# Strassen's scheme in the output projection of a hybrid streaming encoder layer

## The chip, the cores and the metric

The kernel runs on one core of one Trainium2 chip. The metric is the device time of an execution in microseconds (us). All arithmetic is float32: each operand of a large product is split into a high half (its cast to the type float32r) and a low half (what the cast leaves), and TensorE multiplies high by high, low by high and high by low. A product of a 128 x 128 stationary tile with 512 columns therefore takes three matmuls.

## The reference, cut to what matters

One layer works on 2048 prompt tokens and 64 sample tokens of width 1024. Three groups of heads (HGRN2 of width 1024, retention of width 512, attention to a memory of width 512) give `mixed`, whose width is 2048. What the change touches is the end of the layer:

```python
    mixed = jnp.concatenate([o_hg, o_rt, o_xa], axis=-1)      # (tokens, 2048)
    out = x.astype(f32) + mixed @ w_out.astype(f32)           # w_out (2048, 1024)
...
y_prompt = rms_norm(hp, final_norm_g)   # hp: out of the prompt tokens
y_sample = rms_norm(hs, final_norm_g)   # hs: out of the sample tokens
```

## The kernel before, in words

**Order of the work.** The kernel projects the normalised tokens to all heads (helpers `gemm_col`, whose matmuls are line 249, and `gemm_tok`, line 294), works through the head groups, and writes each gated group to a DRAM buffer `mixT` (2048 features x 2112 tokens). Last among the groups is the attention to the memory, `xa_heads`; its products are lines 741, 763 and 785, and its gates lines 422 and 423. The output projection follows. Two engines run in exactly the order in which the program is written: TensorE, and SyncE, which issues all loads and stores. For the others a scheduler puts instructions in order; those written under `tc.high_priority` are drawn forward.

**A clock of its own.** `pe(us)` counts TensorE's time in the program, and `poll()` issues the steps of background generators whose time has come. `store(dst, src)` is such a task: its DMA (line 127) is placed in SyncE's queue 4.5 us, by this count, after the call.

**Weights.** `wsrc` lists 512 KB slabs (128 x 1024). `w_fetch` loads a slab into one of three buffers `st` (line 141), `w_pump` splits it (`split`, lines 240 and 241: ScalarE casts the high half, VectorE subtracts for the low one) into a pair of buffers `whi`, `wlo`, or, for the output projection, also into the buffers `ha` and `hb`, which held normalised tokens. `worder` assigns the 16 slabs of `w_out` to these: five to `whi`/`wlo`, four to `ha`, four to `hb`, and the rest to `whi`/`wlo` and eight small buffers. All of `w_out`, both halves, stays in the core's memory while the output runs. `allow["a"]` opens `ha` during the last attention head, `allow["b"]` opens `hb` after it.

**The output stage.** For each of 16 chunks of 128 tokens (and the sample's 64 before the last one) `y_load` splits the chunk's 16 tiles of `mixT` as stationary operands (four splits of 512 columns) and loads x. `y_half` runs once for each half of the output's columns: 16 contraction tiles x 3 terms = 48 matmuls (line 1159) into one bank of PSUM, then VectorE adds x (line 1168) and ScalarE squares and sums (line 1169). The two norms' sums give a factor per token, with GpSimd's power in between, and VectorE scales by it and by `final_norm_g` (lines 1182 and 1185). `mix_fetch` (line 1005) asks for the next chunk's `mixT` between the two halves, and x follows (line 1030). For the sample the high and low halves stand side by side in one stationary tile, so that a product needs two matmuls: 64 in all.

Of the kernel before, what the change touches and what calls it, by code (L numbers as in the profile page):

```python
# [15 lines left out]
P = 128  # L16
# [18 lines left out]
E_OFF = [0, 128, 224, 288]  # L35

# [27 lines left out]
def layer_kernel(ctx: ExitStack, tc: tile.TileContext, io: dict):  # L64
# [6 lines left out]
    mvd = tc.dram_tile([NMEM, 512], F32, name="mvd")  # L71

# [22 lines left out]
    def task(cls, gen, delay):  # L95
        prev = last.get(cls)
        t = {"t": now[0] + delay, "gen": gen, "prev": prev, "stage": 0}
        last[cls] = t
        pend.append(t)
# [34 lines left out]
    wpos = {"dma": 0, "split": 0, "credit": 0, "ahead": 1}  # L134
    allow = {}

    def w_fetch(now_=0):
        while wpos["dma"] < min(len(wsrc), wpos["split"] + max(now_, wpos["ahead"])):
            i = wpos["dma"]
            wst[i] = stp.tile([P, 1024], F32, tag="st", name="wst")  # L140
            dma(wst[i], wsrc[i][0])
            wpos["dma"] += 1

    def w_pump():
        while wpos["split"] < len(wsrc):
            i = wpos["split"]
            n, tag = wsrc[i][1:]
            if tag == "w":
                if not wpos["credit"]:
                    break  # L150
                wpos["credit"] -= 1
                hi = wpool.tile([P, 1024], F32R, tag="whi", name="whi")
                lo = wpool.tile([P, 1024], F32R, tag="wlo", name="wlo")
            elif tag == "v":
                if tag not in allow:
                    break
                w_fetch()
                parts_ = [[vpool.tile([P, 512], F32R, tag="v", name="v") for _ in range(2)] for _ in range(2)]
                st = wst.pop(i)
                for k in range(2):  # L160
                    split(parts_[0][k], parts_[1][k], st[:, k * 512:(k + 1) * 512])
                wt[i] = parts_
# [3 lines left out]
            else:  # L166
                if tag not in allow:
                    break
                if not allow[tag]:
                    allow[tag] += [allow_alloc(tag), 0]  # L170
                (hi_, lo_), j = allow[tag]
                allow[tag][1] += 1
                hi, lo = hi_[:, j * 1024:(j + 1) * 1024], lo_[:, j * 1024:(j + 1) * 1024]
# [5 lines left out]

    def allow_alloc(tag):  # L180
        return [t.rearrange("p k n -> p (k n)") for t in h_tile(tag)]
# [14 lines left out]
    cst = const.tile([P, 396], F32, name="cst")  # L196
# [5 lines left out]
    ones = const.tile([P, P], F32, name="ones")  # L202
# [15 lines left out]
    s_prompt = [const.tile([P, P], F32, name=f"sp{h}") for h in range(8)]  # L218
# [4 lines left out]
    def small(n, tag):  # L223
        return sm.tile([P, n], F32, tag=tag, name=tag, bufs=2 if n == 32 else 3)
# [501 lines left out]
    def att_tail(h, tok0, nt, kv_p, kv_s, qh, ql, sh):  # L726
# [48 lines left out]
        po = acc()  # L775
# [70 lines left out]
    n_in = len(wsrc)  # L846
    worder = [(0, i, "w") for i in range(4)] + [(0, i, "a") for i in range(4, 8)] + [(1, 0, "w")]
    worder += [(1, i, "b") for i in range(1, 5)] + [(1, 5, "w"), (1, 6, "v"), (1, 7, "v")]
    wsrc += [(io["w_out_t"][half, i], 512, tag) for half, i, tag in worder]
# [146 lines left out]
    def mix_fetch(o, L, early):  # L996
        out = []
        for q in range(0, 4, 1 if early else 2):
            if early:
                m = vpool.tile([P, 512], F32, tag="v", name="mv").rearrange("p (k l) -> p k l", k=4)  # L1000
                n = 1
            else:
                m = stp.tile([P, 1024], F32, tag="st", name="mst").rearrange("p (k l) -> p k l", k=8)
                n = 2
            dma(m[:, :, 0:L], mixT[q * 512:(q + n) * 512, o:o + L].rearrange("(k p) l -> p k l", p=P))
# [280 lines left out]
```

## Time and profile before

| | |
|---|---|
| median of 3 runs | 1949.01 us (1948.51 to 1950.47) |
| profiled execution | 1948.53 us, span 1946.7 us |
| granted TensorE clock, mean | 0.993 |
| TensorE matmuls busy | 1912.0 us (98%), 10938 |
| VectorE busy | 1043.7 us (54%) |
| ScalarE busy | 586.5 us (30%) |
| GpSimd busy | 140.6 us (7%) |
| DMA | 153.21 MB, mean 79 GB/s |

The span is the time from the first to the last instruction that the profiler recorded; the execution's own time is 1.8 us longer. In the profile PE is TensorE's matmuls, PEld its weight loads, DVE VectorE, ACT ScalarE, POOL GpSimd, SP SyncE. A row such as `L1159 PE MATMUL acc<-whi,s` names the line of the kernel, the engine, and the output and the inputs by the program's names. A number in brackets at its end is the idle time ahead of it and what ended it. The share of the DMA engines is the mean over the core's 16.

### The profile page before, as it was taken

Reading aid. Unit: us, or ns where it says so; the run is one execution under the profiler, and the core shown is the slowest. Engines: PE = TensorE matmul, PEld = TensorE weight load, DVE = VectorE, ACT = ScalarE, POOL = GpSimd, SP = SyncE. Lnnn points to the kernel's source line nnn. Section 1 sums busy time; section 2 is a strip of 40 time slices with the busy share of each in tenths; the row PEclk is TensorE's granted clock in tenths of the full one; section 3 lists DMA queues with packets and bytes.
Section 4 is the critical chain, followed back from the end, with each engine's and each line's share of the span. In section 5 each row is a group of like instructions: output and inputs, shape, how many; then the busy total and the mean of one; then the engine's idle time right before and its main releaser. Section 6 shows DMA issues by size and latency. Waiting matters only on the chain.

```text
span 1946.7 us, 28118 instructions
## 1 busy us (share of the span) xinstructions
PE 1912.0 (98%) x10938; PEld 1620.4 (83%) x10938; DVE 1043.7 (54%) x2512; ACT 586.5 (30%) x1414; POOL 140.6 (7%) x335
## 2 busy tenths in 40 slices
PE   8999999999999999999999999999999999999998
PEld 7888788888888787987789998899988978888886
DVE  7616547762767546417737775477765652222222
ACT  6412232232233434412323332233334431111111
POOL 0000100000100100000101111021100000000000
PEclk8999999999999999999999999999999999999999
DMA  7512211111111413411311111111122352233322
GB/s 253 172 59 55 81 55 52 63 44 49 44 44 60 147 60 121 126 54 49 96 48 46 53 49 49 44 49 49 60 71 73 104 162 87 87 100 110 93 71 60
DMA packets 116742, 153.21 MB, mean 79 GB/s; under 512 B 13312, under 2 KB 79232, under 8 KB 116608
## 3 DMA queue, kind: packets, MB, share of 16 engines
q1 hardware_dynamic: 116608, 151.41, 25.3%
q8 instruction: 86, 1.41, 0.3%
q14 instruction: 48, 0.39, 0.1%
HBM read 117.69 MB, written 33.69 MB: 78 GB/s over the span
## 4 chain that ended last, share of the span: by engine, by line
PE 88%; DVE 5%; DMA 2%; ACT 2%; issue 1%; POOL 1%; SPq 0%; DVEq 0%; POOLq 0%; ACTq 0%
PE acc L249 39%; PE acc L1159 19%; PE acc L294 16%; PE scb L522 2%; PE ob L531 2%; PE ob L563 1%; PE ob L566 1%; PE acc L264 1%; PE acc L785 1%; PE ob L741 1%; DVE wlo L241 1%; PE tr L516 1%; PE tr L763 1%; PE tr L581 1%; POOL rs L237 0%
## 5 line engine op out<-in xcount | busy, mean ns | idle before, releaser
L249 PE MATMUL acc<-hb,whi 128*128 128x320 f32 (+2 forms) x1696 | 410.8, 332 | 0.4 <-DVE hb L371 0.4
L249 PE MATMUL acc<-ha,whi 128*128 128x512 f32 x1120 | 353.2, 396 | 0.0
L249 PEld LDWEIGHTS acc<-hb,whi 128*128 128x128 f32 x1696 | 285.8, 190 | 25.3 <-issue 4.4
L241 DVE TENSOR_TENSOR wlo<-wst,whi 128x1024 fp32r<-128x1024 f32 x118 | 143.8, 1226 | 266.3 <-ACT whi L240 265.3
L249 PE MATMUL acc<-hb,wlo 128*128 128x256 f32 (+2 forms) x848 | 277.7, 327 | 0.0
L249 PEld LDWEIGHTS acc<-ha,whi 128*128 128x128 f32 x1120 | 204.2, 188 | 41.1 <-issue 2.6
L249 PE MATMUL acc<-ha,wlo 128*128 128x512 f32 x560 | 219.4, 392 | 0.0
L240 ACT CAST whi<-wst 128x1024 fp32r<-128x1024 f32 x118 | 122.8, 1051 | 209.7 <-PE acc L249 172.0
L249 PEld LDWEIGHTS acc<-hb,wlo 128*128 128x128 f32 x848 | 160.9, 190 | 11.3
L294 PE MATMUL acc<-whi,ha 128*128 128x512 f32 x512 | 161.5, 397 | 0.0
L294 PE MATMUL acc<-whi,hb 128*128 128x512 f32 x512 | 160.0, 394 | 0.0
L1159 PE MATMUL acc<-whi,s 128*128 128x512 f32 x396 | 125.8, 396 | 1.3 <-ACT s L240 1.0
L249 PEld LDWEIGHTS acc<-ha,wlo 128*128 128x128 f32 x560 | 105.3, 188 | 22.7
L294 PEld LDWEIGHTS acc<-whi,hb 128*128 128x128 f32 x512 | 94.5, 188 | 19.8 <-issue 1.2
L294 PEld LDWEIGHTS acc<-whi,ha 128*128 128x128 f32 x512 | 94.1, 189 | 19.6 <-issue 1.3
L294 PE MATMUL acc<-wlo,ha 128*128 128x512 f32 x256 | 100.1, 391 | 0.0
L294 PE MATMUL acc<-wlo,hb 128*128 128x512 f32 x256 | 99.8, 390 | 0.0
L1159 PE MATMUL acc<-ha,s 128*128 128x512 f32 x400 | 96.3, 396 | 0.0
L1159 PE MATMUL acc<-hb,s 128*128 128x512 f32 x400 | 96.2, 396 | 0.0
L241 DVE TENSOR_TENSOR s<-mst,s 128x512 fp32r<-128x512 f32 (+1 forms) x64 | 40.4, 672 | 97.2 <-ACT s L240 97.2
L1159 PEld LDWEIGHTS acc<-whi,s 128*128 128x128 f32 x396 | 74.3, 188 | 19.6 <-ACT s L240 1.3
L1159 PEld LDWEIGHTS acc<-ha,s 128*128 128x128 f32 x400 | 75.0, 188 | 18.2
(234 smaller groups left out, 2915.5 us busy)
## 6 DMA issues: line engine op xcount, KB each, us to landing
wst<-w_in_t SPq DMA_DIRECT2D x104, 512.0 KB, 3.8
mixT<-s SPq DMA_DIRECT2D x64, 256.0 KB, 4.2
mst<-mixT SPq DMA_DIRECT2D x30, 512.0 KB, 5.7
wst<-w_out_t SPq DMA_DIRECT2D x16, 512.0 KB, 4.0
xq<-x_prompt SPq DMA_DIRECT2D x18, 256.0 KB, 4.9
o_yp<-xq SPq DMA_DIRECT2D x18, 256.0 KB, 2.1
s<-mixT SPq DMA_DIRECT2D x16, 256.0 KB, 3.1
s<-x_prompt SPq DMA_DIRECT2D x16, 256.0 KB, 5.1
```

Source lines behind the costliest of these rows:

```text
L240: S.copy(hi, src)
L241: V.tensor_tensor(out=lo, in0=src, in1=hi.bitcast(F32), op=ALU.subtract)
L249: T.matmul(ps[:, 0:nt], w[a][:, kk, :], ht[b][:, kk, 0:nt], start=(n == 0), stop=(n == 23))
L264: T.matmul(ps[:, 0:nt], w[a][:, kk, :], ht[b][:, kk, 0:nt], start=(kk == 0 and a + b == 0), stop=(kk == KT - 1 and a == 1))
L294: T.matmul(ps[0:L, :], ht[b][:, kk, o:o + L], w[a][:, kk % 2, :], start=(n == 0), stop=(n == 23))
L516: T.transpose(trk[:, c * 128:(c + 1) * 128], kch[:, c * 128:(c + 1) * 128], ident)
L522: T.matmul(scb[32 * e:32 * e + 32, c * 128 + 32 * e:(c + 1) * 128], K[:, c * 128 + 32 * e:c * 128 + 32 * e + 32], Qe[:, c, E_OFF[e]:E_OFF[ ...
L531: T.matmul(db[:, c * 128:(c + 1) * 128], kT[:, c * 128:(c + 1) * 128], vt[c], start=True, stop=True)
L563: T.matmul(ob[:, c * 128:(c + 1) * 128], A[:, c * 128:(c + 1) * 128], vt[c], start=True, stop=first)
L566: T.matmul(ob[:, c * 128:(c + 1) * 128], qst[:, c * 128:(c + 1) * 128], st[c][0], start=False, stop=True)
L581: T.transpose(tro[:, c * 128:(c + 1) * 128], on[:, c * 128:(c + 1) * 128], ident)
L1159: T.matmul(ps, m[a][:, kk % 4], w[b], start=(n == 0), stop=(n == 16 * len(terms) - 1))
```

## The change

**What it computes.** The contraction of 2048 is taken in two passes p of 1024. In each pass the token chunks of 128 are taken in pairs. A pair's operand is a matrix of 2 x 2 blocks: a11 and a12 are the two halves (512 each) of the first chunk's contraction, a21 and a22 those of the second chunk. The weights of the pass are B11, B12, B21, B22 (512 x 512 each). Then

```
S1 = a21 + a22   S2 = S1 - a11   S3 = a11 - a21   S4 = a12 - S2
T1 = B12 - B11   T2 = B22 - T1   T3 = B22 - B12   T4 = B21 - T2
P1 = a11 B11  P2 = S2 T2  P3 = S1 T1  P4 = S3 T3  P5 = a12 B21  P6 = a22 T4  P7 = S4 B22
y11 = P1 + P5            y12 = P1 + P2 + P3 + P7
y21 = P1 + P2 + P4 + P6  y22 = P1 + P2 + P3 + P4
```

Each product is 4 contraction tiles x 3 terms = 12 matmuls. They are made in the order B11, T2, T1, T3, B21, T4, B22 (named by the weight block). The sample uses B11, T1, B21, B22, 32 matmuls a pass. The sequence is 8 pairs and the sample in the first pass, then 7 pairs, the sample and the last pair in the second.

**What it moves.** The first pass starts from x, its sums go to a new DRAM buffer `yd`, and the second pass reads them back and does norm, scaling and output. Only one pass's weight blocks fit. Those of the first are built from the slabs at the end of the attention (the functions `o_...`, called by `w_pump`). Those of the second are built during the first pass by `w2_steps`, some seven steps in each pair from the second on: a slab is loaded, blocks are subtracted, and high and low halves of 512 columns go through two pairs of small buffers `wbuf` to DRAM, `wcd`. `w2_load` loads each block from there when the last pair of the first pass, or its sample, has read the same block of the first pass for the last time: T2, T3 and T4 in the last pair, B11, T1, B21 and B22 in the sample. Smaller edits go with it: one product of the last attention head goes to another PSUM bank, `cst` and `ones` become one tile, and so do the eight `s_prompt`, so that x and the sums find room there.

The core of the diff, with the lines of the new kernel that the prediction speaks of named behind it:

```diff
 def w_fetch(now_=0):
-        while wpos["dma"] < min(len(wsrc), wpos["split"] + max(now_, wpos["ahead"])):
+        lim = wpos["split"] + max(now_, wpos["ahead"])
+        if wpos["hold"] is not None:
+            lim = min(lim, wpos["hold"] + 3)
+        while wpos["dma"] < min(len(wsrc), lim):
...
+    def t2_unit(region, u, z, t1):
+        hi, lo = out_unit(region, "T2", u)
+        v2 = [vpool.tile([P, 512], F32, tag="v", name="t2") for _ in range(2)]
+        for k in range(2):
+            c = slice(k * 512, (k + 1) * 512)
+            sub(v2[k], z[:, c], t1[:, c])
+            split(hi[:, c], lo[:, c], v2[k])
+        live["T2", u] = v2
...
+    def o_b21(u):
+        def f(i, x):
+            split(*out_unit("b", "B21", u), x)
+            v2 = live.pop(("T2", u))
+            for k in range(2):
+                c = slice(k * 512, (k + 1) * 512)
+                sub(x[:, c], x[:, c], v2[k])
+            split(*out_unit("b", "T4", u), x)
...
-    nxt = y_load(0, raw0)
     allow["b"] = []
-    allow["v"] = []
     w_pump()
...
+    def a_prep(raw, tmp=None):
+        a11, a12, a21, a22 = raw
+        s1, s2, s4 = tmp or [vpool.tile([P, 512], F32, tag="v", name="as") for _ in range(3)]
+        A = {"B11": part(a11)}
+        vadd(s1, a21, a22)
+        yield A
+        sub(s2, s1, a11)
+        A["T2"] = part(s2)
+        yield A
...
+    def w2_steps():
+        for u in range(2):
...
+            def out(blk, x):
+                for k in range(2):
+                    c = slice(k * 512, (k + 1) * 512)
+                    hi, lo = wbuf[wb[0] % 2]
+                    wb[0] += 1
+                    S.copy(hi, x[:, c])
+                    V.tensor_tensor(out=lo, in0=x[:, c], in1=hi.bitcast(F32), op=ALU.subtract)
+                    yield
+                    dma(wcd[blk][u, 0][:, c], hi.bitcast(F32))
+                    dma(wcd[blk][u, 1][:, c], lo.bitcast(F32))
+
+            x, y, z = load("B11"), load("B12"), load("B22")
+            yield
+            sub(y, y, x)
+            sub(z, z, y)
+            sub(x, z, x)
+            yield
+            yield from out("T3", x)
+            yield from out("T1", y)
+            v = load("B21")
+            yield
+            sub(v, v, z)
+            yield from out("T2", z)
+            yield from out("T4", v)
+            for blk in ("B11", "B21", "B22"):
+                x = load(blk)
+                yield
+                yield from out(blk, x)
+
+    def w2_load(blk):
+        for u in range(2):
+            for i in range(2):
+                dma(wo[blk, u][i].bitcast(F32), wcd[blk][u, i])
...
+        prod(Z, "T1", A["T1"], True, True)
+        with hp():
+            vadd(r[3], r[3], Z)
+            vadd(r[1], r[1], Z)
+        if 0 < n < len(seq) - 1:
+            r_next = r_fetch_next()
+        prep()
...
+        if last1:
+            w2_load("T4")
```

In the new kernel `sub` is line 168, `vadd` line 1207, the two halves of `split` lines 314 and 315, the matmuls of `prod` line 1252, the low halves of `w2_steps` line 1272, the loads of `w2_load` line 1298, `mixT` is asked for on line 1080, and all other stores are line 130.

Three places in the order of the engines. First VectorE, where the output stage starts; before, the last gate of the attention (`s<-s,acc`) and the first token splits (`s<-mv,s`) stand so:

```order
L241 TENSOR_TENSOR wlo<-wst,whi 128x1024
L241 TENSOR_TENSOR s<-acc,s 128x320
L423 SCALAR_TENSOR_TENSOR s<-s,acc 128x320
L241 TENSOR_TENSOR s<-mv,s 128x512
L241 TENSOR_TENSOR hb_14563<-wst,hb_14562 128x1024
L241 TENSOR_TENSOR s<-mv,s 128x512
```

And now, with the first and the second product's token splits at the end (`sp_all` holds S2):

```order
L315 TENSOR_TENSOR wlo<-wst,whi 128x1024
L497 SCALAR_TENSOR_TENSOR s<-s,acc 128x320
L315 TENSOR_TENSOR hb_14554<-wst,hb_14553 128x1024 x2
L168 TENSOR_TENSOR wst<-wst,t_14117 128x512
L168 TENSOR_TENSOR wst<-wst,t_14118 128x512
L168 TENSOR_TENSOR wst<-wst,t_14371 128x512
L168 TENSOR_TENSOR wst<-wst,t_14372 128x512
L315 TENSOR_TENSOR wlo<-wst,whi 128x1024
L315 TENSOR_TENSOR hb_14554<-wst,hb_14553 128x1024 x2
L315 TENSOR_TENSOR s<-mv,s 128x512
L315 TENSOR_TENSOR s<-sp_all,s 128x512 x2
```

The splits of the last slabs (B21 into `hb`, B22 into `wlo`) and the four subtractions for T4 have come to stand between the gate and the first token split; before, one `hb` split stood behind it.

Second VectorE in the middle of the output stage; before, one chunk's rows follow the other's (L241 token splits, L1168 adds, L1182 and L1185 norm and scaling):

```order
L241 TENSOR_TENSOR s<-mst,s 128x512 x4
L1168 TENSOR_TENSOR xq<-xq,acc 128x512 x2
L1182 TENSOR_TENSOR rs_15347<-ss_15220 128x1
L1185 SCALAR_TENSOR_TENSOR xq<-xq,rs_15347,q2b_138 128x512
L1185 SCALAR_TENSOR_TENSOR xq<-xq,rs_15347,q2b_139 128x512
L241 TENSOR_TENSOR s<-mst,s 128x512 x4
L1168 TENSOR_TENSOR abuf_109<-abuf_109,acc 128x512
L1168 TENSOR_TENSOR abuf_111<-abuf_111,acc 128x512
```

And now in the first pass, from the add of the fifth pair's third product (T1) on; `wst` are slabs of the second pass, `hb` and `q2b` the buffers `wbuf`, `abuf` and `m` the sums, `as` and `mv` token blocks:

```order
L1207 TENSOR_TENSOR xq<-xq,acc 128x512
L168 TENSOR_TENSOR wst<-wst 128x1024 x3
L1272 TENSOR_TENSOR hb_14553<-wst,hb_14553 128x512
L1272 TENSOR_TENSOR q2b_138<-wst,hb_14554 128x512
L1272 TENSOR_TENSOR hb_14553<-wst,hb_14553 128x512
L1207 TENSOR_TENSOR abuf_116<-abuf_116,m_15432 128x512
L315 TENSOR_TENSOR s<-mv,s 128x512
L1207 TENSOR_TENSOR m_15432<-m_15432,acc 128x512
L1207 TENSOR_TENSOR abuf_116<-abuf_116,tr 128x512
L1207 TENSOR_TENSOR abuf_118<-abuf_118,m_15432 128x512
L1207 TENSOR_TENSOR as<-mv 128x512
L1207 TENSOR_TENSOR abuf_118<-abuf_118,acc 128x512
```

Three wide subtractions and three low halves of weights stand ahead of the token split `s<-mv,s` of the same pair.

Third SyncE. Before, the middle of the output stage repeats this, loads of the next chunk and stores of the one before:

```order
L1030 DMA abuf_111<-x_prompt 128x512
L127 DMA o_yp<-xq 128x512 x2
L1005 DMA mst<-mixT 128x8x128 x2
L1030 DMA xq<-x_prompt 128x512 x2
L127 DMA o_yp<-abuf_109 128x512
L127 DMA o_yp<-abuf_111 128x512
```

Now, between the passes, from the last load of T4 (`wcT_66`) to the first of T1 (`wcT_63`); `wcB_61` is B11, and `yd` the sums:

```order
L1298 DMA hb_14554<-wcT_66 128x1024
L130 DMA yd<-sp_all 128x512
L130 DMA yd<-cst 128x512
L1487 DMA q2b_138<-final_norm_g 128x512
L1487 DMA q2b_139<-final_norm_g 128x512
L1080 DMA mv<-mixT 128x4x128 x4
L1298 DMA whi<-wcB_61 128x1024
L1298 DMA wlo<-wcB_61 128x1024
L1298 DMA whi<-wcB_61 128x1024
L1298 DMA wlo<-wcB_61 128x1024
L130 DMA yd<-r_120 128x512
L1298 DMA whi<-wcT_63 128x1024
```

What stands between one pair's last rows and the next one's first are now loads of weights (512 KB each), with four loads of `mixT` and the stores of sums among them.

More of the change, by code (lines that the diff above doesn't have):

```diff
@@ L35 @@
 E_OFF = [0, 128, 224, 288]
+BLOCKS = ("B11", "T2", "T1", "T3", "B21", "T4", "B22")
 HP = 250
@@ L774, in att_tail @@
         gs = sh["gs"]
-        po = acc()
+        po = obank() if tok0 >= 1024 and h == 3 else acc()
         np_ = min(nt, SEQ - tok0)
@@ L1151, in y_half @@
-    def y_half(mx, x, ss, L, half):
-        ps = acc()
-        n = 0
-        for kk in range(16):
-            w = wo[half, kk]
-            m = mx[kk // 4]
-            terms = ((0, 0), (1, 0), (0, 1)) if L == P else ((0, 0), (0, 1))
-            for a, b in terms:
-                T.matmul(ps, m[a][:, kk % 4], w[b], start=(n == 0), stop=(n == 16 * len(terms) - 1))
-                n += 1
+    fg = [q2b[i].rearrange("p a b -> p (a b)") for i in range(2)]
+    b_hi, b_lo = allow["b"][0]
+    wbuf = [[b_hi[:, 4096:4608], b_hi[:, 4608:5120]], [b_lo[:, 4096:4608], fg[0].bitcast(F32R)]]
@@ new lines, in vadd, with k4, part @@
+    def vadd(out, a, b):
+        V.tensor_tensor(out=out, in0=a, in1=b, op=ALU.add)
+    def k4(t):
+        return t.rearrange("p (k l) -> p k l", k=4)
+    def part(x):
+        h, lo = slot(F32R), slot(F32R)
+        split(h, lo, x)
+        return k4(h), k4(lo)
+    def a_prep(raw, tmp=None):
[7 more added lines that the diff above has]
+        yield A
+        A["T1"] = part(s1)
+        sub(a21, a11, a21)
+        yield A
+        A["T3"] = part(a21)
+        sub(s4, a12, s2)
+        yield A
+        A["B21"] = part(a12)
+        yield A
+        A["T4"] = part(a22)
+        yield A
+        A["B22"] = part(s4)
+        yield A
@@ new lines, in s_prep, with prod @@
+    def s_prep(raw):
+        A = []
+        for x in raw:
+            hl = k4(slot(F32R))
+            xv = k4(x)[:, :, 0:DEC]
+            split(hl[:, :, 0:DEC], hl[:, :, DEC:P], xv)
+            A.append(hl)
+        yield A
+    def prod(bank, blk, op, start, stop, terms=((0, 0), (1, 0), (0, 1))):
+        for kt in range(4):
+            u, k = kt // 2, kt % 2
+            for j, (a, b) in enumerate(terms):
+                T.matmul(bank, op[a][:, kt], wo[blk, u][b][:, k * 512:(k + 1) * 512],
+                         start=start and kt + j == 0, stop=stop and kt == 3 and j == len(terms) - 1)
@@ L1161, in y_half @@
                 pe(0.213)
             poll()
[L1163 to L1186 removed]
+    wb = [0]
```

365 lines of the change are left out of this document (268 added, 97 removed).

## The prediction

> **What bounds the kernel now.** I read the page first: the span, and three rows of its 40 slices.
>
> ```profile
> span 1946.7 us, 28118 instructions
> PE   8999999999999999999999999999999999999998
> DVE  7616547762767546417737775477765652222222
> DMA  7512211111111413411311111111122352233322
> ```
>
> TensorE (PE) is at nine tenths or more almost throughout. VectorE (DVE) stands mostly at 5 to 7 tenths and falls to 2 in the last eight slices, the output projection; the DMA engines are at 2 to 3 there. Next, the chain of waits in order of time (start, length, what) gives that stage's end.
>
> ```profile
> 1578.65 360.82 PE acc L1159 x1546
> 1939.50 0.70 DVE xq L1168
> 1942.08 0.75 DVE xq L1185
> ```
>
> 1546 matmuls run without a gap: 360.82 / 1546 = 0.2334 us each. From the last of them, at 1939.5, 7.2 us of add, norm, scaling and store remain. Last, the busy times over the undisturbed part of the stage:
>
> ```profile
> core 0: us, PE busy (x) PEld busy (x) DVE busy (x) ACT busy (x) POOL busy (x), PEclk, DMA share, GB/s
> 1624.80:1900.00 275.20, 275.20 (x1181) 221.57 (x1180) 64.41 (x108) 44.55 (x98) 8.82 (x24) 1.00 0.30 89
> ```
>
> VectorE works 64.41 of 275.2 us (23%), ScalarE 16%, the DMA engines 0.30. TensorE alone is the bound; all else has room. The profiled execution took 1948.5 us (the span and 1.8 around it), 0.5 below the median of the three runs, 1949.0. I sum against 1948.5.
>
> **The change, part by part.** *Matmuls.* Before: 16 chunks x 2 halves x 48, and 64 for the sample: 1600. After: 8 pairs x 2 passes x 7 products x 12, and 64: 1408. 192 fewer x 0.2334 = **-44.8 us**. A product now lasts 12 x 0.2334 = 2.8 us and a pair 19.6 us in each pass. That is the beat for what follows.
>
> *VectorE.* Two wide splits, and two of 512 columns with an add behind them:
>
> ```profile
> 1543.48 2.35 DVE L241 TENSOR_TENSOR ha<-wst,ha 128x1024 fp32r<-128x1024 f32 x2
> ...
> 1802.24 1.29 DVE L241 TENSOR_TENSOR s<-mst,s 128x512 fp32r<-128x512 f32 x2 [0.50 <-ACT s L240]
> 1803.45 0.68 DVE L1168 TENSOR_TENSOR xq<-xq,acc 128x512 f32<-128x512 f32 x1
> ```
>
> The narrow ones and the add start (1803.45 - 1802.24) / 2 = 0.61 apart, the wide ones take 2.35 / 2 = 1.17. A pair needs 11 adds of products, 4 token sums and 7 splits: 22 x 0.61 = 13.4 us. The weights of the second pass add 28 x 0.61 + 8 x 1.17 = 26.4 us over some six pairs, 4.4 each: 17.8 of 19.6 us. It fits, at 91% where it was 23%, and only while nothing at the head of its queue waits.
>
> *DMA.* Windows in which the DMA engines were full (columns as above), two with long rows, one with the 512-byte runs of mixT:
>
> ```profile
> 8.00:10.00 2.00, 2.00 (x18) 2.00 (x16) 2.00 (x6) 1.71 (x5) 0.00 (x0) 1.00 1.03 419
> 14.00:16.00 2.00, 2.00 (x19) 2.00 (x19) 1.50 (x3) 1.34 (x2) 0.00 (x0) 1.00 1.05 390
> 1535.00:1536.00 1.00, 1.00 (x5) 0.79 (x6) 0.79 (x2) 0.47 (x2) 0.00 (x0) 1.00 0.96 268
> ```
>
> I take 395 GB/s for long rows (0.66 us for 256 KB, 1.33 for a 512 KB slab) and 268 for mixT (0.98 for 256 KB). A pair of the first pass moves 4 pieces of mixT (3.9 us), 4 of x and 4 of y (5.3). The weight work is 14 slabs and 56 half stores, 55.6 us, nearly all in the second to sixth pairs, 11.1 each. Together 20.3 us in 19.6: full. Two more rows: SyncE's issue of four loads, and the stores of y, whose last column is the time from issue to landing.
>
> ```profile
> 1531.95 2.13 SPq L1005 DMA_DIRECT2D mv<-mixT  x4
> ```
>
> ```profile
> o_yp<-xq SPq DMA_DIRECT2D x18, 256.0 KB, 2.1
> ```
>
> Four loads take SyncE 2.13 us, so some 24 rows a pair 13 of 19.6: hidden. A store lands 2.1 us after its issue, 1.4 more than the 0.66 of its transfer.
>
> *Start of the stage.* VectorE before (the last gate, the first token split), and TensorE's waits there:
>
> ```profile
> 1557.86 0.49 DVE L423 SCALAR_TENSOR_TENSOR s<-s,acc 128x320 f32<-128x320 f32 x1 [1.43 <-ACT s L422]
> 1558.37 0.69 DVE L241 TENSOR_TENSOR s<-mv,s 128x512 fp32r<-128x512 f32 x1
> ```
>
> ```profile
> 1559.12 0.50 PE L1159 MATMUL acc<-whi,s 128*128 128x512 f32 x1 [0.23 <-DVE s L241]
> 1565.67 0.50 PE L785 MATMUL acc<-s 128*128 128x256 f32 x2 [0.35 <-DVE s L241]
> 1577.56 1.09 PE L785 MATMUL acc<-s 128*128 128x256 f32 x8 [1.33 <-DVE s L241]
> ```
>
> The output began at 1559.1 and lost 0.35 and 1.33 later. Now five wide operations and four block subtractions stand between gate and token split: 5 x 1.17 + 4 x 0.61 = 8.3 us, and 0.4 for ScalarE's halves. TensorE stops at its second matmul, with the rest of the attention behind it, 8.7 longer. The later 1.7 go, as that rest is then ready: **+7.0** (from 4, if VectorE finds some of it done early, to 9, if slabs land late).
>
> *First pass, fifth to seventh pair.* In the fifth pair, timed from its first product, the third product ends at 8.4 and VectorE's add behind it at 9.1. Next in its queue are the three wide subtractions. SyncE could ask for their slabs only after a store whose low half VectorE makes 2 us after the end of the pair before; three slabs, behind that pair's sums on the same queue, land from about 11.5 to 13. Subtractions until 15.3, two low halves until 17; the third writes the buffer of the first, which must be stored: 20. The token split after that waits for mixT, asked for behind those stores: 22.8. The T2 split of the next pair is 14 operations on, about 32.5 with one more wait for mixT; TensorE wanted it at 22.6, so 10 lost. The sixth pair loses 1 in the same way; the seventh has the last slab (B22) behind half stores once more and loses 7. **+18.** The trace has no VectorE queue this full in the stage, so I bound it: 5 if the slabs come in time, 35 if five pairs lose 7 each; I take the reckoned value.
>
> *Between the passes.* 28 slabs, 37.2 us of transfer, each block asked for when its last reader is done. Timed from the end of the eighth pair: T4's are asked for at -2.8 and in by 3.5; y 1.3, gain 1.3 and mixT 3.9 follow on the queue: 10.0; B11 takes 5.3 and, like a store, about 1 to land: 16.3. The sample's 32 matmuls end at 7.5: 8.8 idle. T1 costs 0.4, B21 (behind y and four sums read back) 3.0: 12.2. The mixT of the next pair comes last, at 40; ten VectorE operations on, its T2 is split 4 late, and its T1 another 1.9 behind four scalings. **+18** (12 without that aftermath; 30 at 297 GB/s, the 89 of the stage divided by its share of 0.30).
> The Trainium skill, page "DMA: Bandwidth & Descriptors", section "Specifications", gives about 358 GB/s as one core's share of HBM. By that the 28 slabs would take an estimated 41 us; the 419 above exceeds it, so the row stands.
>
> *The clock.* The trace has one idle of such a length. TensorE's rows around it, and the windows (granted clock third from the right):
>
> ```profile
> 41.03 1.22 PE L264 MATMUL acc<-ha,whi 128*128 128x512 f32 x2 [2.93 <-ACT whi L240]
> 44.16 1.05 PE L264 MATMUL acc<-ha,whi 128*128 128x512 f32 x2
> 48.35 0.62 PE L264 MATMUL acc<-ha,whi 128*128 128x512 f32 x2
> ```
>
> ```profile
> 39.00:40.00 1.00, 0.00 (x0) 0.00 (x0) 0.98 (x2) 0.82 (x3) 0.94 (x1) 1.00 1.01 377
> 41.00:42.00 1.00, 0.97 (x2) 0.50 (x2) 0.99 (x1) 0.51 (x1) 0.00 (x0) 0.50 0.05 20
> 45.00:46.00 1.00, 1.00 (x4) 0.79 (x3) 1.00 (x2) 0.89 (x3) 0.00 (x0) 0.50 0.17 53
> 48.00:49.00 1.00, 1.00 (x6) 0.83 (x5) 0.96 (x3) 1.00 (x2) 0.00 (x0) 1.00 0.00 0
> ```
>
> After 2.93 us of idle the clock was 0.50 for about 6 us; two matmuls took 1.05 us instead of 0.62. That is 3 us lost. My reckoning has six idles of 3 us or more: at the start, two about the end of the fifth pair, in the seventh, and two between the passes. Half of the loss falls into waits that come anyway: 6 x 3 / 2, about **+8** (0 to 17).
> The Trainium skill, page "TensorE: Matmul & The Clock Gate", section "HAM oscillation — how this bites in real kernels", warns of idles over about 3.4 us: each puts the clock at half until another such stretch of work. By that an estimate is 1.7 us a gap; the row's 3 is more, at a shorter idle.
>
> The end is the chain of before, 7.2 us. *Sum:* -44.8 + 7.0 + 18 + 18 + 8 = +6.2, so 1948.5 + 6.2 = 1954.7, **1955 us**. The ends of all bounds: -44.8 + 4 + 5 + 12 + 0 = -24, and -44.8 + 9 + 35 + 30 + 17 = +46.
>
> **The rivals.**
> *The queues hold in the first pass (faster).* If the three slabs of the fifth pair land by 9 us into it, the subtractions follow the add at once, their low halves end before 14, when the fifth product is due, and the seventh pair recovers too. The 18 go, and about half of the clock's 8: 1955 - 22 = **1933**. For it: 17.8 of 19.6 us fits on VectorE, and the excess of the DMA engines is only 0.7 a pair. Against it: SyncE takes its queue in order, and the slabs stand behind a store that VectorE makes late.
> *The DMA engines are slower than their best windows.* At 297 GB/s the 8 MB of such a pair take 27 us, 7.4 over 19.6; five pairs 37, and 30 between the passes: -44.8 + 7 + 37 + 30 + 8 = +37, **1986**. For it: reads of mixT, stores and loads are mixed, as in the stage that gave 89 at 0.30. Against it: the full windows above.
>
> **How the numbers follow.** My case, with waits in both places: 0.48, itself from 1943 to 1972, since its two terms of 18 can each be 8 off. Queues hold: 0.38, from 1915 to 1945. Slow DMA: 0.14, above 1970. A measurement of this kernel can tell about 0.2% from no change, 3.9 us. Within that lie 0.15, all from my case; faster 0.38; slower 0.33 + 0.14 = 0.47. The range is 1925 to 1980: it leaves out the lower third of the faster case and half of the slow one, 0.13 + 0.07.
>
> **What would show it.** Each step has its place in the new profile: 84 matmuls a pair at 0.233 us; the first token split about 8.7 us later after the last gate; VectorE near 90% in the first pass, with waits of TensorE for it at the ends of the fifth and seventh pairs; an idle of about 9 us behind the sample's matmuls that ends with the landing of B11; slices with a granted clock below 1 behind these. I am wrong if the second to eighth pairs of the first pass (7 x 19.6 = 137 us of matmuls) take less than 145 us or more than 175, if the idle behind the sample is under 4 us, or if TensorE waits mostly for mixT instead of for the splits.

## The result and the profile after

The changed kernel takes 1962.55 us (median of 4 runs, 1961.47 to 1965.10) against 1948.99 us before (4 runs, 1948.51 to 1950.47): the ratio is 1.007, interval 1.0058 to 1.0081, 13.6 us slower. The forecast was 1955. The profiled execution took 1962.26 us, 13.7 more than that of before, and its span is 1960.5.

First the page of the changed kernel, the rows that answer to those of before and the granted clock:

```profile
span 1960.5 us, 28531 instructions
PE   8999999999999999999999999999999799887998
DVE  7517457753677557327547773687755886755986
PEclk9999999999999999999999999999999899888999
DMA  7511211111112423222211111121222468799543
```

In the last nine slices VectorE and the DMA engines have filled, as they should, but TensorE has holes now, and its clock falls below nine tenths where the holes are. Then the windows of the two stretches that lost, and the rest of the second pass (length, busy time of PE, PEld, DVE, ACT and POOL, granted clock, DMA share, GB/s):

```profile
1592.20:1757.45 165.25, 149.45 (x590) 116.86 (x588) 116.45 (x185) 46.02 (x83) 0.00 (x0) 0.93 0.84 277
1757.45:1826.10 68.65, 54.58 (x201) 40.85 (x200) 38.25 (x64) 18.77 (x39) 2.26 (x6) 0.88 0.85 291
1815.00:1952.00 137.00, 136.50 (x585) 109.37 (x583) 111.23 (x190) 49.60 (x111) 10.92 (x28) 1.00 0.44 136
```

The first row is the second to eighth pair of the first pass: 7 x 19.6 = 137.2 us of matmuls took 165.2. TensorE was idle for 15.8 us of it, and busy for 12.2 more than 137.2, at a mean clock of 0.93. The second row is what lies between the passes, the sample and the first two pairs of the second pass: 200 matmuls, 46.7 us, took 68.7, with 14.1 idle and 7.9 for the clock. The rest of the second pass runs at full clock. Last, the waits of TensorE themselves:

```profile
1555.93 0.49 PE L1252 MATMUL acc<-whi,s 128*128 128x512 f32 x1 [3.81 <-ACT s L314]
1564.19 0.79 PE L1252 MATMUL acc<-whi,s 128*128 128x512 f32 x1 [7.76 <-DVE s L315]
1677.10 1.52 PE L1252 MATMUL acc<-whi,s 128*128 128x512 f32 x2 [4.64 <-ACT s L314]
1686.18 0.80 PE L1252 MATMUL acc<-whi,s 128*128 128x512 f32 x1 [3.32 <-ACT s L314]
1729.49 0.50 PE L1252 MATMUL acc<-whi,s 128*128 128x512 f32 x1 [3.20 <-ACT s L314]
1736.87 0.50 PE L1252 MATMUL acc<-whi,s 128*128 128x512 f32 x1 [2.26 <-ACT s L314]
1770.37 1.19 PE L1252 MATMUL acc<-whi,s 128*128 128x512 f32 x2 [5.29 <-DMA whi<-wcB]
1788.01 0.76 PE L1252 MATMUL tr<-hb,s 128*128 128x512 f32 x2 [3.96 <-DMA hb<-wcB]
1805.87 0.80 PE L1252 MATMUL acc<-whi,s 128*128 128x512 f32 x1 [3.81 <-ACT s L314]
```

They stand near the places of the forecast: at the start, at the end of the fifth pair (the sixth begins at 1677.1) and in the sixth, at the end of the seventh (the eighth begins at 1729.5) and in the eighth, at B11 (1770), B21 (1788) and the T2 of the pair behind (1806). A stretch of half clock follows each; the two at the start share one.

From the last matmul of the attention's projections (its end is at 1557.4 before and at 1552.1 after) the difference adds up so:

| part | us |
|---|---|
| up to that matmul | -5.2 |
| 192 matmuls fewer | -44.8 |
| from there to the second pair (40.1 us; 14.6 of waits and clock, 2.9 before) | +11.7 |
| second to eighth pair | +28.0 |
| sample and two pairs between the passes | +22.0 |
| rest of the second pass | +1.2 |
| tail behind the last matmul (8.2 for 7.2) | +1.0 |
| sum | +13.9, against 13.7 measured |

How much of the -5.2 is the change's is not known: in eleven profiled executions of kernels whose program is the same up to there (the changed kernel and all experiments but e1 and e10), that matmul ended anywhere from 1552.1 to 1555.2. All of these are ahead of the 1557.4 of before, but of before there is one trace.

### The profile page after: what moved, and what is told of

Read it like the earlier page. It is cut to its first block, busy times and chain, and to the rows that moved or that the text cites. A ratio compares the mean times of both kernels' runs of the same rounds, so it can differ in the third digit from the quotient of the medians.

```text
span 1960.5 us, 28531 instructions
## 1 busy us (share of the span) xinstructions
PE 1884.6 (96%) x10746; PEld 1592.4 (81%) x10746; DVE 1236.0 (63%) x2822; ACT 637.3 (33%) x1510; POOL 139.9 (7%) x335
## 4 chain that ended last, share of the span: by engine, by line
PE 70%; DVE 13%; DMA 7%; ACT 3%; issue 3%; POOL 1%; SPq 1%; DVEq 0%; POOLq 0%; ACTq 0%
PE acc L323 37%; PE acc L368 15%; DMA mv<-mixT 3%; PE acc L1252 2%; PE scb L596 2%; PE ob L605 1%; PE ob L637 1%; DMA wst<-w_out_t 1%; PE ob L640 1%; DVE s L315 1%; PE ob L1252 1%; PE acc L338 1%; PE ob L815 1%; POOL rs L311 1%; DVE wlo L315 1%
## 5 line engine op out<-in xcount | busy, mean ns | idle before, releaser
L1252 PE MATMUL acc<-whi,s 128*128 128x512 f32 x276 | 100.7, 438 | 37.5 <-ACT s L314 21.2
L368 PEld LDWEIGHTS acc<-whi,hb 128*128 128x128 f32 x512 | 94.5, 188 | 19.7 <-issue 1.2
L1252 PEld LDWEIGHTS acc<-whi,s 128*128 128x128 f32 x276 | 57.3, 209 | 58.5 <-ACT s L314 24.7
L1099 ACT COPY v<-acc 128x512 f32<-128x512 f32 x48 | 28.2, 587 | 194.2 <-PE acc L368 194.2
L311 POOL TENSOR_TENSOR rs<-rs,nhalf 128x4 f32<-128x4 f32 (+4 forms) x74 | 64.0, 866 | 6.1
L496 ACT ACTIVATE s<-acc 128x512 f32<-128x512 f32 (+2 forms) x60 | 31.3, 521 | 101.3 <-PE acc L323 101.2
L1252 PE MATMUL acc<-wlo,s 128*128 128x512 f32 x148 | 63.0, 426 | 0.0
```

What stands on the lines that cost most here:

```text
L311: G.tensor_tensor(out=out, in0=out, in1=nhalf[0:out.shape[0], 0:n], op=ALU.pow)
L368: T.matmul(ps[0:L, :], ht[b][:, kk, o:o + L], w[a][:, kk % 2, :], start=(n == 0), stop=(n == 23))
L496: S.activation(gs[:, 0:nt], ps[:, 0:nt], AF.Tanh, scale=0.5)
L1099: S.copy(v, ps)
L1252: T.matmul(bank, op[a][:, kt], wo[blk, u][b][:, k * 512:(k + 1) * 512], start=start and kt + j == 0, stop=stop and kt == 3 and j == len(te ...
```

## The experiments

Totals carry that scatter, so each kernel is read by its three stretches as well, taken from the starts of TensorE's products: "start" is from the end of the projections to the second pair, "pairs" the second to the eighth, "between" the sample and two pairs. The nine kernels below whose program at the start is that of the changed kernel (e3 to e9, e11, e12) took 38.1 to 39.6 us there, the changed kernel 40.1. "Between", the changed kernel, e1, e3, e6, e7 and e11 took 68.7 to 71.2. A difference inside these bounds may be scatter.

| kernel | median | start | pairs | between |
|---|---|---|---|---|
| changed kernel | 1962.5 | 40.1 | 165.2 | 68.7 |
| e1_start | 1962.7 | 37.0 | 165.9 | 70.3 |
| e2_warm | 1962.9 | 36.0 | 163.5 | 72.0 |
| e3_noprep | 1935.5 | 38.1 | 137.2 | 71.2 |
| e4_noreload | 1942.4 | 38.2 | 165.2 | 46.7 |
| e5_ahead | 1942.0 | 38.5 | 137.2 | 76.4 |
| e6_nostore | 1935.2 | 38.4 | 137.2 | 68.9 |
| e7_novec | 1949.8 | 38.4 | 151.3 | 69.8 |
| e8_border | 1963.9 | 38.7 | 164.8 | 71.2 |
| e9_keep | 1931.7 | 38.3 | 137.2 | 66.9 |
| e10_all | 1927.6 | 34.3 | 137.2 | 66.4 |
| e11_seven | 1950.2 | 38.3 | 152.8 | 70.5 |
| e12_spread | 1945.6 | 39.6 | 137.2 | 80.8 |

### Which part of the change costs what: e3 and e4

```diff
 e3_noprep
-        for u in range(2):
+        for u in range(1):
...
-            x, y, z = load("B11"), load("B12"), load("B22")
...
-            for blk in ("B11", "B21", "B22"):
+            for blk in ("B11",):
...
-                dma(wo[blk, u][i].bitcast(F32), wcd[blk][u, i])
+                dma(wo[blk, u][i].bitcast(F32), wcd["B11"][0, i])
 e4_noreload
     def w2_load(blk):
+        return
```

> Leaves out the preparation of the second pass's weights, all but one slab; the second pass loads that slab's halves for every block, so its sums aren't those of the reference. The reload keeps its size. Theory (VectorE's queue in the sixth and the eighth pair waits for late slabs and for buffers that are being stored, and mixT stands behind those stores): the waits of the first pass from the fifth pair's end on go, 15.8 us, and the two stretches of half clock behind them, some 9: about 1937. Rival (the token loads alone are late, since mixT comes at 268 GB/s): at most a third of it goes, 1954 or more.

> Leaves out the reload between the passes: the second pass uses the first pass's blocks, so its sums aren't those of the reference. Preparation and stores stay. Theory (the 28 slabs fill the DMA engines, B11 and B21 land late, and mixT of the next pair behind them): idles of 5.3, 4.4 and 4.2 us go, and three stretches of half clock, some 6: about 1942. Rival (the sums read back from DRAM and mixT would be late anyway): only the 5.3 and 4.4 go, with 4 of clock: 1948 or more.

Measured: 1935.5 (1933.55 to 1937.57) and 1942.4 (1937.65 to 1944.83). The windows of the pairs in the first, and of the stretch between the passes in the second:

```profile
1592.60:1729.80 137.20, 137.20 (x590) 109.96 (x589) 92.15 (x149) 30.65 (x52) 0.00 (x0) 1.00 0.59 188
```

```profile
1757.30:1804.00 46.70, 46.70 (x201) 37.40 (x200) 38.64 (x65) 17.92 (x37) 1.86 (x4) 1.00 0.65 198
```

In both rows PE's busy time is the whole window, at full clock. So the 28.0 of the first pass go with the preparation of the second pass's weights, and the 22.0 between the passes with the reload; mixT, x and the sums alone are on time. Both theories hold, with the totals forecast (1937 and 1942).

### What in the preparation: e6, e7, e5, e11, e12

```diff
 e6_nostore
-                    dma(wcd[blk][u, 0][:, c], hi.bitcast(F32))
-                    dma(wcd[blk][u, 1][:, c], lo.bitcast(F32))
+                    if (blk, u) == ("T3", 0):
+                        dma(wcd[blk][u, 0][:, c], hi.bitcast(F32))
+                        dma(wcd[blk][u, 1][:, c], lo.bitcast(F32))
 e7_novec
-                    V.tensor_tensor(out=lo, in0=x[:, c], in1=hi.bitcast(F32), op=ALU.subtract)
...
-            sub(y, y, x)
-            sub(z, z, y)
-            sub(x, z, x)
```

> Leaves out 54 of the 56 half stores of prepared weights; the reload reads one pair of halves for every block, so the second pass's sums aren't those of the reference. Slabs, subtractions and halves stay. Theory of late slabs and of buffers that wait for their store: the second part goes, the three slabs of the fifth pair still come late: 10 to 15 of the 28 are left, about 1948. Rival 1 (the DMA engines are too full): all goes, 1936. Rival 2 (VectorE is too full): hardly anything goes, 1958 or more.

> Leaves out VectorE's share of the preparation (8 subtractions and 28 low halves, 26 us); ScalarE's casts are stored in their place, so the second pass's sums aren't those of the reference. Slabs, casts, stores and reload stay in number and size. Theory of late slabs and buffers: ScalarE's queue waits for them as VectorE's did, and mixT still stands behind the stores: 10 to 18 of the 28 are left, about 1950. Rival 1 (VectorE is too full): all goes, 1936. Rival 2 (the DMA engines are too full): over 20 are left, 1956 or more.

Measured: 1935.2 (1931.88 to 1936.79) and 1949.8 (1948.34 to 1950.99). The windows of the pairs, without stores and without VectorE's share:

```profile
1593.60:1730.80 137.20, 137.20 (x589) 110.54 (x588) 115.84 (x186) 46.84 (x83) 0.00 (x0) 1.00 0.73 234
```

```profile
1591.60:1742.90 151.30, 142.93 (x589) 113.02 (x588) 91.46 (x150) 43.32 (x77) 0.00 (x0) 0.97 0.92 305
```

Without the stores all 28 go, although VectorE has its whole work (115.84 of 137.2 us, 84%). VectorE's time is not the limit. The number is that of rival 1, but it doesn't show that the DMA engines were too full. The theory took it that the three slabs of the fifth pair would still come late, and in this run they did not: with fewer stores to wait for, SyncE asked for them 7.4 us into the fourth pair instead of 7.2 us into the fifth.

```profile
1640.24 1.58 SPq L1263 DMA_DIRECT2D wst<-w_out_t  x3
```

Bytes, buffers in store and the progress of SyncE's queue all change at once in e6. In e7, with the stores but 25 us of VectorE's work less, 14.1 are left, as its theory had it (10 to 18).

The next three kernels keep all work and bytes and only move it. Two edits, together in e5 and apart in e11 (slabs ahead) and e12 (five steps a pair):

```diff
 e5_ahead and e11_seven: each slab as soon as its buffer is free
-            v = load("B21")
-            yield
-            sub(v, v, z)
-            yield from out("T2", z)
-            yield from out("T4", v)
...
+            yield from out("T3", u, x)
+            v = load("B21", u)
+            yield from out("T1", u, y)
+            l0 = load(*nxt_[0])
+            sub(v, v, z)
+            yield from out("T2", u, z)
+            l1 = load(*nxt_[1])
+            yield from out("T4", u, v)
+            l2 = load(*nxt_[2])
 e5_ahead and e12_spread: no step ahead of T3 and of B22
+    SKIP = [3, 6]
...
     def step():
+        place[0] += 1
+        if n and (place[0] - 1) % 7 in SKIP:
+            return
         next(steps, None)
```

> Every slab of the second pass's weights is asked for when its buffer comes free, at least two products ahead of its use (the second half's subtractions follow the first half's directly, the blocks without subtraction come last), with five steps a pair instead of seven. Work and bytes are unchanged. In the changed kernel the second to eighth pairs of the first pass took 165.2 us, 28 more than their matmuls; without the preparation 137.2. Theory (slabs that are asked for too late stand at the head of VectorE's and ScalarE's queues): at most 8 of the 28 are left, about 1942. Rival (VectorE at over nine tenths, or the DMA engines, are simply full): over 20 are left, 1955 or more.

> Slabs asked for ahead, as in the kernel that took 1942.0, but with seven steps of preparation in each pair as in the changed kernel, so that it is done in 33 steps by the fifth pair instead of spread over six. Theory (the late slabs alone cost the 28): the second to eighth pairs still take at most 145 us, total about 1943. Rival (it was the spreading, VectorE at over nine tenths otherwise): 150 us or more, 1950 or more.

> The changed kernel with its order of slabs, but five steps of preparation in a pair instead of seven: the other half of what the kernel with 1942.0 does. Its second to eighth pairs took 137.2 us, those of the changed kernel 165.2, and with slabs ahead but seven steps 152.8. Theory 1 (late slabs and a preparation packed too densely each cost about half): 12 to 18 of the 28 left, about 1949. Theory 2 (the density is the whole cause, and asking ahead only helped where the queues were full): at most 5 left, 1940. Theory 3 (three slabs at once come late however the steps lie): 20 or more left, 1955 or more.

Measured: 1942.0 (1941.44 to 1945.34), 1950.2 (1948.94 to 1953.11), 1945.6 (1943.15 to 1950.79). The windows of the pairs in e5 and in e12:

```profile
1592.50:1729.70 137.20, 137.20 (x590) 110.54 (x589) 116.09 (x185) 46.74 (x83) 0.00 (x0) 1.00 0.96 314
```

```profile
1592.50:1729.70 137.20, 137.20 (x590) 110.54 (x588) 114.70 (x183) 45.62 (x81) 0.00 (x0) 1.00 0.95 313
```

Five steps instead of seven take away all 28 of the pairs, with the slabs in their old order: theory 2 of e12. Its total (1940) was missed, for a reason at the border that follows below. Asking ahead alone takes away 12.4 (e11's rival). e5 met its forecast of 1942, but the reason given for it was the lesser one.

Were the DMA engines too full in the changed kernel? Its windows (columns as above) for the second to fourth, the fifth and the eighth pair, and for four microseconds inside the fifth:

```profile
1592.24:1651.04 58.80, 58.80 (x253) 47.38 (x252) 45.56 (x74) 18.96 (x34) 0.00 (x0) 1.00 0.84 278
1651.04:1677.10 26.06, 20.30 (x85) 15.52 (x83) 16.41 (x25) 7.23 (x13) 0.00 (x0) 0.98 0.66 221
1729.49:1757.45 27.96, 24.81 (x85) 18.95 (x85) 19.29 (x32) 4.61 (x9) 0.00 (x0) 0.82 0.99 330
1666.00:1668.00 2.00, 2.00 (x10) 1.64 (x9) 1.91 (x2) 0.00 (x0) 0.00 (x0) 1.00 0.07 27
1668.00:1670.00 2.00, 2.00 (x11) 1.59 (x10) 1.77 (x2) 0.12 (x1) 0.00 (x0) 1.00 0.00 0
```

The second to fourth pairs, with seven steps each, lost nothing. The fifth, the first to lose, has the lowest share of all, and just ahead of TensorE's wait the DMA engines had nothing to do. How that came, the rows of the fifth pair show, which began at 1651.0. SyncE's issue of three slabs, then VectorE's rows:

```profile
1658.23 2.67 SPq L1263 DMA_DIRECT2D wst<-w_out_t  x3
```

```profile
1666.06 3.74 DVE L168 TENSOR_TENSOR wst<-wst 128x1024 f32<-128x1024 f32 x3 [3.26 <-DMA wst<-w_out_t]
1673.36 0.69 DVE L1272 TENSOR_TENSOR hb<-wst,hb 128x512 fp32r<-128x512 f32 x1 [1.54 <-DMA wcT<-hb]
1677.08 0.69 DVE L315 TENSOR_TENSOR s<-mv,s 128x512 fp32r<-128x512 f32 x1 [2.42 <-ACT s L314]
```

SyncE's and ScalarE's rows for the tokens of the sixth pair:

```profile
1672.61 2.44 SPq L1080 DMA_DIRECT2D mv<-mixT  x4
1676.43 0.62 ACT L314 CAST s<-mv 128x512 fp32r<-128x512 f32 x1 [2.70 <-DMA mv<-mixT]
```

VectorE stood for a slab (3.26). SyncE meanwhile stood from 1660.9 to 1670.5 for the first high half of T3, which ScalarE could cast only behind VectorE's subtractions. MixT for the sixth pair stands behind that store in SyncE's queue and so was asked for at 1672.6; the cast and the token split, which TensorE waited for, came last. SyncE's waits for ScalarE's halves over the seven pairs (us in total, times, longest), in the changed kernel and in e12:

```profile
SPq L1274 <- ACT hb L1271: 36.1, 8, 9.5
```

```profile
SPq L1274 <- ACT hb L1271: 6.9, 6, 1.8
```

In e12 the same three slabs are asked for no earlier, 7.4 us into the fifth pair (it began at 1651.3). But with five steps the subtractions stand one product later in the queue, they start 16.3 us into the pair with no wait ahead of them, and mixT is asked for ahead of T3's stores, at 1668.6:

```profile
1658.65 1.77 SPq L1263 DMA_DIRECT2D wst<-w_out_t  x3
```

```profile
1667.60 1.22 DVE L168 TENSOR_TENSOR wst<-wst 128x1024 f32<-128x1024 f32 x1
```

So what cost time in the fifth pair is three engines waiting for each other in turn. The bytes can explain little of the 28: the changed kernel moved 277 GB/s x 165.25 us = 45.8 MB in the seven pairs. e12 ran at 313 GB/s with a share of 0.95, 329 at full share. At that rate, an estimate, 45.8 MB take 139 us, 2 more than the matmuls. How the loss of the later pairs divides among slabs, buffers and full DMA engines (share 0.99 in the eighth) is not shown.

### Where the gain is given back: between the passes

With e5 and e12 the first pass gains 28, but "between" grows from 68.7 to 76.4 and 80.8. The wait for B11 is the longest of all in both, and in e5 SyncE takes 8.26 us for two loads that read back sums, 6.6 of them waiting for a store of these sums, with B21's and B22's loads behind it (TensorE's rows in e5 and e12, then SyncE's in e5):

```profile
1750.48 1.19 PE L1252 MATMUL acc<-whi,s 128*128 128x512 f32 x2 [13.16 <-DMA whi<-wcB]
```

```profile
1754.31 1.19 PE L1252 MATMUL acc<-whi,s 128*128 128x512 f32 x2 [16.98 <-DMA whi<-wcB]
```

```profile
1753.05 8.26 SPq L1203 DMA_DIRECT2D sp_all<-yd  x2
```

That TensorE comes to the border 28 us earlier is not enough to cause it: e3 and e6 reach it as early (1729.8 and 1730.8), and their "between" is 71.2 and 68.9. What e5 and e12 have besides is a preparation that ends late. SyncE issues its last store 27 us ahead of the border in the changed kernel, 8 ahead in e5 (1721.9) and 10 behind it in e12 (1739.6, the border is at 1729.7). SyncE's first load of B11 (in e6 the block that stands for it), in the changed kernel, e6 and e12:

```profile
1763.92 1.39 SPq L1298 DMA_DIRECT2D whi<-wcB  x1
```

```profile
1737.48 1.64 SPq L1299 DMA_DIRECT2D whi<-wcT  x1
```

```profile
1746.75 2.67 SPq L1298 DMA_DIRECT2D whi<-wcB  x1
```

It is issued 6.5 us after the border in the changed kernel and 6.7 in e6, but 17.0 in e12 (and 14.4 in e5). So spreading the preparation has put part of it in the way of the reload: e12 moves 22.8 MB between the passes (282 GB/s x 80.8 us), the changed kernel 20.0.

Three kernels went at this border. e8 (on the changed kernel) reorders the products of the second pass's first pair; e9 (on e5) begins the second pass with the pair whose sums are still in their buffers; e10 adds two moves on SyncE's queue and the start.

```diff
 e8_border
+        if n == n1 + 1:
+            X = acc()
+            prod(X, "T2", A["T2"], True, True)
...
+            prod(W, "T3", A["T3"], True, True)
...
+            prod(Y, "T4", A["T4"], True, True)
...
+            prod(X, "B11", A["B11"], True, True)
...
 e9_keep
-    seq += [(1, i * 256, P) for i in range(7)] + [(1, SEQ, DEC), (1, 7 * 256, P)]
+    seq += [(1, 7 * 256, P)] + [(1, i * 256, P) for i in range(6)] + [(1, SEQ, DEC), (1, 6 * 256, P)]
...
-            r_next = r_fetch_next()
+            r_next = rset[1] if n == n1 else r_fetch_next()
...
-            else:
+            elif not last1:
                 put(o + P, P, r[2], 0)
 e10_all, in addition to e9_keep and to the edit of e1_start
         if last1:
+            raw9 = raw_fetch(*seq[n + 2])
             w2_load("T2")
...
-            for i in range(2):
-                dma(fg[i], io["final_norm_g"][i * 512:(i + 1) * 512].partition_broadcast(P))
...
                 w2_load("B22")
+                for i in range(2):
+                    dma(fg[i], io["final_norm_g"][i * 512:(i + 1) * 512].partition_broadcast(P))
```

> The first pair of the second pass takes its products in the order T2, T3, T4, B11, T1, B21, B22, the order in which the reload brings them. In the changed kernel the sample and the first two pairs of that pass took 68.7 us for 46.7 of matmuls; without the reload 46.7. Theory (B11 and B21 are missed while T2, T3 and T4 lie ready): 8.4 us of products cover the wait for B11, and that for B21 goes: 10 to 13 of the 22 are left, about 1952. Rival (the DMA engines have a fixed amount to move, and the mixT of the pair behind comes last): the wait moves to that pair, over 17 are left, 1958 or more.

> On the kernel with the slabs asked for ahead (1942.0): the second pass begins with the pair that ended the first, so that its sums stay in their buffers; 4 stores and 4 loads of 256 KB between the passes go. There the sample and two pairs took 76.4 us for 46.7 of matmuls, SyncE stood 8.3 us at reading back sums that were still being stored, with B21's and B22's loads behind it. Theory (a transfer at the head of SyncE's queue): B21's wait of 3.7 goes and B22 and the next mixT come 8 earlier, 6 to 10 of the 29.7 go: about 1934. Rival (the DMA engines are full with the 28 slabs whatever stands in the queue): at most the transfer time of what is left out, and that in B11's shadow: 1939 or more.

> The version to beat both: the former, with the mixT of the second pass's first pair asked for in the last pair of the first pass instead of ahead of B11's load, the gain of the norm asked for behind the reload, and the first pair's token splits ahead of the last slabs. Theory: B11's wait of 13.2 shrinks by the 5 us of transfers that stood ahead of it, the wait for tokens behind it (4.4) goes, and some 3 at the start: about 1922. Rival (the 28 slabs alone fill the time, 37 to 43 us): 1930 or more.

Measured: 1963.9 (1962.71 to 1964.51), 1931.7 (1931.03 to 1933.05) and 1927.6 (1927.00 to 1929.28). In e8 the wait for B11 became one for tokens, whose T2 needs three of the four pieces of mixT:

```profile
1772.27 0.80 PE L1273 MATMUL acc<-whi,s 128*128 128x512 f32 x1 [7.13 <-ACT s L314]
```

Its theory falls: the product that now comes first waits for mixT, which stands on SyncE's queue behind T4's loads. The total is in its rival's range (24.5 left), but the wait moved to this pair's tokens, not to the pair behind. e9's theory holds: "between" goes from 76.4 to 66.9, and the wait for B21 is gone. That it also moves 2.1 MB less is not separated from the order of the queue. e10 lies between its two cases: the moves take little more off "between" (66.4), since B11 is still missed for 9.10 us; the start gives 4.0.

```profile
1725.00:1791.40 66.40, 52.58 (x201) 39.88 (x200) 35.59 (x60) 18.51 (x39) 2.25 (x6) 0.87 0.87 310
1741.70 1.19 PE L1255 MATMUL acc<-whi,s 128*128 128x512 f32 x2 [9.10 <-DMA whi<-wcB]
```

e10 is the version to keep: against before its ratio is 0.9889 (0.9873 to 0.9904), 21 us faster, and the 28 slabs between the passes still cost it 19.7.

### The start and the clock: e1 and e2

```diff
 e1_start
+    cur = a_prep(raw0, [spf[:, 0:512], spf[:, 512:1024], r2.rearrange("p a b -> p (a b)")])
+    for _ in range(3):
+        A_next = next(cur)
     allow["b"] = []
     w_pump()
...
-    cur = a_prep(raw_next, rset[1][0:3])
-    for _ in range(3):
-        A_next = next(cur)
 e2_warm
+    def fill(bank, n, blk):
+        w = wo["T3", 0][0]
+        for _ in range(FILL.get((n, blk), 0)):
+            T.matmul(bank, w[:, 0:128], w[:, 0:512], start=True, stop=True)
```

> The three token splits of the first pair are written ahead of the last slabs of weights. The changed kernel took 1962.3 in its profiled execution; TensorE stood there 3.8 and 7.8 us idle about its first product and ran about 6 us at half clock behind it. Theory (those waits are VectorE's queue: five wide operations and four subtractions ahead of the token split): the 7.8 go, with the 0.9 later and the 2.7 us that the clock costs behind them: about 1952. Rival (the weights that now come later are missed instead, by the fifth product or by the rest of the attention): the wait only moves, 1959 or more.

> Adds 141 matmuls without use, of about 0.233 us, at the eight places where TensorE stood idle for 2 us or more, each filling some 0.85 of its wait; they depend on nothing late. Theory (each idle is followed by 4 to 6 us at half clock, about 2.4 us lost each, 19 in all, and shorter idles aren't): clock at 1.00 through the output, waits as before, about 1945. Rival 1 (the half clock comes from the load on the chip or from a schedule, not from the idles): 1960 to 1965. Rival 2 (what the half clock loses falls into waits that come anyway, since VectorE and the DMA engines set the beat there): the waits grow by as much, 1955 or more.

Measured: 1962.7 (1956.98 to 1966.01) and 1962.9 (1959.53 to 1964.19), no change in either. In e1 the start took 37.0 us, 1.1 less than the shortest of the kernels with the old start and 3.1 less than the changed kernel, not 10. The wait moved to the T3 of the first pair, whose token split now stands behind the last splits of weights:

```profile
1560.29 0.50 PE L1255 MATMUL acc<-whi,s 128*128 128x512 f32 x1 [0.92 <-DVE s L315]
1580.47 5.04 PE L1255 MATMUL ob<-ha,s 128*128 128x512 f32 x11 [3.15 <-DVE s L315]
```

So the wait only moved, as the rival had it. In e2 the clock did not stay at 1.00 everywhere, since waits of about 2.4 us were left. The mean clock rose from 0.982 to 0.990. The start is 4.1 shorter (2.1 less than the shortest with the old start), the pairs only 1.7, and "between" is 3.3 longer (0.8 above its scatter). The total is the same: what the fuller clock gave came back as waiting. That is rival 2, as far as this run, with half clock not fully removed, can say.

## Why the prediction was right, and where it was not

The sign, the mechanism and the places of the waits were right, and the sum was 7.5 us short of the median. That it came so near is in part luck: the three terms of idle were 43 together and measured 39.4, the clock cost 14 more than forecast, and 5.2 us ahead of the output stage, which no term has, went the other way. Step by step:

- *Matmuls, -44.8.* Right: 200 matmuls took 46.70 us in e4, 0.2335 each.
- *VectorE fits, at 91%.* Right that it fits: it worked 84% of the window in e6 and TensorE lost nothing.
- *DMA, 395 GB/s, 20.3 us a pair.* **The rate was too high, but it is not what cost the time.** It came from windows with long rows alone. Over the mixed traffic of the first pass it was 313 GB/s at a share of 0.95 (e12), 329 at full share. The Trainium skill, page "DMA: Bandwidth & Descriptors", section "Measured (HBM→SBUF, 128 partitions, SWDGE, issued from GpSimd)", lists 341 GB/s for transfers of 1 MB. The windows of long rows here, 390 to 419, lie above it and the mixed traffic below, and these measurements decide. The bytes were too many as well: the terms give 12 x 0.262 + 4.4 = 7.5 MB a pair (not the 8 of the rival with slow DMA engines), but the second to fourth pairs moved 5.5 each, and lost nothing. In that rival five pairs lose alike; here the fifth lost first, at a share of 0.66.
- *Start, +7.0.* The token split came 9.1 us after the last gate, 8.6 more than before (8.7 forecast). These are VectorE's rows of the gate and the split:

```profile
1554.32 0.48 DVE L497 SCALAR_TENSOR_TENSOR s<-s,acc 128x320 f32<-128x320 f32 x1
1563.45 0.69 DVE L315 TENSOR_TENSOR s<-mv,s 128x512 fp32r<-128x512 f32 x1
```

  But the gate itself was late behind a slab (2.2 us after the projections' last matmul, 0.5 before), so TensorE's idle was 9.5 longer than before, and the clock added some 2.
- *First pass, +18.* 15.8 of idle. This is the step whose mechanism the runs bear out, the queues that wait for each other. The places were right: the three slabs, the buffer in store, the token split behind them, at 15.0, 22.3 and 26.0 us of the fifth pair (13, 20 and 22.8 forecast). In the fifth and sixth pairs TensorE was idle for 9.4 us (10 and 1 forecast), in the seventh and eighth for 6.4 (7). One sign named for being wrong was TensorE waiting mostly for mixT. By the profile its waits end with token splits, but at the end of the fifth pair the split had itself waited for mixT, as the prediction's chain had it.
- *Between the passes, +18.* 14.1 of idle: 5.3 for B11 (8.8 forecast), 4.4 for B21 (3.4 for T1 and B21), 4.4 for the next pair (4 and 1.9).
- *Clock, +8.* **Mis-sized**: 12.2 and 7.9 in the two stretches and about 2 at the start, 22 in all. There were nine idles of over 2 us, at eight places, not six, and the half of the loss that was to fall into waits did not. e2 suggests, though, that this is no separate price: what its fuller clock gave came back as waiting.
- *The rival in which the queues hold*, 1933, is what e12 does in the first pass, though not by the condition given: its slabs were asked for no earlier. It needed two steps a pair fewer, and "between" then grew by 12.1 of the 28.

Open: how the loss of the sixth to eighth pairs divides; whether a third pair of the buffers `wbuf`, or stores issued by another engine than SyncE, would let seven steps a pair through (no run tried either); what B11's 9.1 us in e10 would need; and whether the small edits of the change have a part in the 5.2 us ahead of the output stage.

## What to carry to other kernels

Work that is moved into a stage where engines have room should be costed by the slot in which it runs and by the queues that it passes. Here everything fitted over the whole pass, but seven steps a pair from the second to the sixth pair cost 28 us, and five steps a pair cost nothing there. When a stage waits, look at the share of the DMA engines in the pair that loses first: they stood empty here, because a store that waited for its data kept the loads behind it from being asked for. And when work is spread, see where its end falls: drawn out to the border between the passes it delayed the reload there, and of the 28 us gained 17 (e12) to 21 (e5) were left in the total.

## What the runs showed of the hardware

- Half clock came after shorter idles than the 2.93 us of before's trace. In e2, TensorE's waits and the clock behind them (third from the right in the window):

```profile
1683.55 0.49 PE L1252 MATMUL acc<-whi,s 128*128 128x512 f32 x1 [2.37 <-ACT s L314]
1684.70 0.54 PE L1252 MATMUL acc<-whi,s 128*128 128x512 f32 x1 [0.66 <-DVE s L315]
```

```profile
1686.00:1688.00 2.00, 2.00 (x6) 1.57 (x5) 1.94 (x3) 0.09 (x1) 0.00 (x0) 0.50 0.83 280
```

  Two idles of 2.37 and 0.66 with one matmul between them were enough, and so were 2.26 and 0.66 in the changed kernel (at 1736.87). The Trainium skill, page "TensorE: Matmul & The Clock Gate", section "HAM oscillation — how this bites in real kernels", names gaps of over about 3.4 us; the measurement decides here.
- The DMA engines ran for 137 us at a share of 0.95 to 0.96 without one wait of TensorE (e5, e12). Nearly full DMA engines cost nothing in that stretch; behind it, at the border, the reload came later.
